# Wide norms at the borders, the norms' weights in front of x's first block, sample softmax one unit later

## The chip, the cores and the metric

The kernel runs on one core of a Trainium2 chip. The metric is the time of one execution on the device in microseconds, as a median of several runs. The profile is of one further execution; its span goes from the first to the last instruction.

Engines are named as in the profile: PE is the matrix engine (PEld its weight loads), DVE the vector engine, ACT the scalar engine, POOL GpSimd, SP the engine that issues most DMAs. An instruction waits in its engine's queue until its operands are ready, and what stands behind it waits too.

## The reference

One inference step of a two-layer encoder with width 1024, for 256 prompt rows and 32 sample rows at once. Each layer has a mixer, a cross-attention into 256 memory tokens and a SwiGLU FFN, each behind an RMSNorm and added to the residual. Cut to what matters here:

```python
def rmsnorm(x, g):
    xf = x.astype(jnp.float32)
    y = xf * lax.rsqrt(jnp.mean(xf * xf, axis=-1, keepdims=True) + RMS_EPS)
    return (y * g.astype(jnp.float32)).astype(x.dtype)

for layer in range(DEPTH):
    ...
    xp = xp + o @ w_out          # o: attention over rmsnorm(xp, g_mix) @ w_in
    xp = xp + memory_attn(rmsnorm(xp, g_xattn[layer]), mk, mv, w_xq[layer], w_xo[layer])
    xp = xp + swiglu(rmsnorm(xp, g_ffn[layer]), w_gate[layer], w_up[layer], w_down[layer])
y_prompt = rmsnorm(xp, g_final)
```

Layer 0's mixer has 8 heads with a relative bias and 8 stick-breaking heads; layer 1's has 16 heads with forget gates. The sample rows attend to caches. All is float32.

## The kernel before

**Layout.** x is held transposed: eight blocks `x[0]` to `x[7]` of 128 features by 288 rows (256 prompt, 32 sample). Every product is made of three fp32r matmuls, because a float32 operand is split into a rounded part and a rest: `hi` and `lo` for weights, `hh` and `hl` for x times the norm's weight (`gain`). ACT makes the rounded part (a CAST, or an ACTIVATE with a scale), DVE the rest. `mm3` issues the three, through `mm` at L68.

**Units.** A unit is one weight tile of 128 x 1024: SP loads it into `st` (4 buffers), ACT casts `hi`, DVE subtracts `lo`, and PE runs 8 x 3 matmuls of 288 columns into one of four accumulators (`acc`, the tile `pj`, `op` or `dn`). Small work (attention, norms, gates) stands between units: generators in `active` are each moved on one step by `tick()` behind a unit, so that a `yield 1` puts what follows it one unit later on PE. Such work uses four other PSUM banks (`att`).

**Norms.** `Norm.add` squares a block on ACT (L251) and adds it up, on POOL but for the last block, which DVE adds (L259). The norm doesn't hold up the projection: PE multiplies the unnormed x, and the result is scaled by `rstd` when it is evacuated. `columns` sums over features with three fp32 matmuls that have the squares as the stationary operand and a column of 1/1024 as the moving one (tile `nrm`), which gives one value per row, rows on partitions; `newton` makes the inverse root of it with 11 DVE instructions of 6 columns (L279 to L284). `rows` spreads it with three fp32 matmuls against `ident` (tile `nr`) over all partitions, and ACT copies it to `rstd` (L331). Evacuations that are asked for earlier wait in `cur.waiting`.

**Borders.** At the border into cross-attention, FFN and layer 1's mixer, `begin` starts two units with the first six blocks of x (18 matmuls each), since the last blocks are still being evacuated. `columns` stands behind the first of the two, and `scale` is a generator that runs `rows` at the first tick.

**Start.** Three weight tiles (`first`, with the blocks in the order of use) and x in four pieces of two blocks (`xh`) are loaded in parts, from SP and ACT's queue; the norms' weights (`gain`, 9 x 8 columns) come in a transfer of their own (L88). PE runs 32 matmuls on an identity (`warm`) meanwhile. `side_by_side` then works on the first three units block by block. Four small constants (`more_constants`) are made on DVE behind the last square.

**Samples and memory.** `attend_sample` makes scores, a softmax (tile `es`), then behind a `yield` transposes it (tile `ts`), and two yields on the result (`os`, `ot`). `Memory.step` makes the memory's keys and values; the values are split into `vh` (ACT) and `vl` (POOL, L371), and the last head's are used in the last attention head of `cross` (tile `xo`).

**End.** The last norm needs no spreading: `columns`, with the squares of the last block summed apart (`hurry`), then transposes `yt`, a scaling by y and the store.

Of the kernel before, what the change touches and what calls it, by code (L numbers as in the profile page):

```python
# [15 lines left out]
P = 128  # L16
# [3 lines left out]
KT = 8  # L20
# [6 lines left out]
def encoder_step(ctx: ExitStack, tc: tile.TileContext, a):  # L27
# [43 lines left out]
    gain = cst.tile([P, 9 * KT], F32, name="gain")  # L71
    xh = [big.tile([P, 2 * NT], F32, tag=f"x{i}", name=f"x{i}") for i in range(4)]
    x = [xh[k // 2][:, (k % 2) * NT:(k % 2) * NT + NT] for k in range(KT)]
# [7 lines left out]
    def x_part(i, eng=DMA):  # L81
        eng.dma_start(xh[i], a["xT"][:, 2 * i * NT:2 * (i + 1) * NT])

    first_part(0, 0, 384)
    x_part(0)
    x_part(1, S)
    x_part(3, S)
    DMA.dma_start(gain, a["gains"])  # L88
    first_part(0, 384, 1024)
    first_part(1, 0, 1024)  # L90
    x_part(2)
    first_part(2, 0, 1024)
# [3 lines left out]
    G.memset(mean1, 1.0 / 1024.0)  # L96
    identb = cst.tile([P, P], BF16, name="identb")
# [3 lines left out]
    line = cst.tile([8, 384], F32, name="line")  # L101
# [38 lines left out]
    def more_constants():  # L140
        V.tensor_scalar(ident, warm[:, 0:P], 1.0 / 32.0, None, op0=ALU.mult)
        by_head = ident.rearrange("p (j i q) -> p j i q", j=2, i=2)
        V.tensor_tensor(fold, by_head[:, :, 0], by_head[:, :, 1], ALU.add)
        V.tensor_tensor(fold4, fold[:, 0, 0:16], fold[:, 1, 0:16], ALU.add)
        V.tensor_copy(ntrir, ntri)
# [95 lines left out]
    class Norm:  # L241
# [7 lines left out]
        def add(self, xb, eng=None):  # L249
# [5 lines left out]
            if self.acc[i] is None:  # L255
                self.acc[i] = q
            else:
                s = tok("ssq")
                eng.tensor_tensor(s[:, :self.n], self.acc[i][:, :self.n], q[:, :self.n], ALU.add)  # L259
                self.acc[i] = s  # L260

        def sum(self, p, part, begin):
            for i, t in enumerate(self.tiles):
                mm(p[:, 2 * i:2 * i + 2], part[:, t:t + 128], mean1, begin and i == 0, False)

        def columns(self, between=None):
            p = att("nrm")
            self.sum(p, self.acc[0], True)
            if between:
                between()  # L270
            if self.acc[1] is not None:
                self.sum(p, self.acc[1], False)
            return self.newton(p)

        def newton(self, p):
            c = len(self.tiles)
            v, y, t = small("ms"), small("y"), small("nt")
            v, y, t = v[:, :2 * c], y[:, :2 * c], t[:, :2 * c]
            V.tensor_scalar(v, p[:, :2 * c], EPS, None, op0=ALU.add)  # L279
            V.tensor_scalar(y.bitcast(I32), v.bitcast(I32), -0.5, 1597463007.0, op0=ALU.mult, op1=ALU.add)  # L280
            for _ in range(3):
                V.tensor_tensor(t, y, y, ALU.mult)
                V.scalar_tensor_tensor(t, t, -0.5, v, op0=ALU.mult, op1=ALU.mult)
                self.last = V.scalar_tensor_tensor(y, t, 1.5, y, op0=ALU.add, op1=ALU.mult)  # L284
            return y

        def rows(self, y):

            p = att("nr")
            for i, t in enumerate(self.tiles):  # L290
                a0 = 256 if i == 2 else t
# [868 lines left out]
```

## Time and profile before

| | us |
|---|---|
| median of 3 runs (957.63 to 958.33) | 957.79 |
| the profiled execution | 958.14 |
| its span | 956.4 |
| PE's idle time in the span (956.4 - 943.6) | 12.8 |
| DVE busy | 587.3 |
| ACT busy | 483.8 |
| POOL busy | 237.2 |

A row of the timeline has the start and the duration of an instruction (or of several that follow each other, xN), its engine, line, operation, output and inputs with their sizes, and in brackets how long the engine was idle before and what ended that. Matmuls overlap, so the cost of one is the distance from one start to the next, not its duration. SPq, POOLq and ACTq are the engines' DMA issues. In the chain of waits a row is start, duration and what held the end up.

### The profile page before, as it was taken

What the parts mean: (1) busy time and instruction counts of PE and PEld (TensorE: products, weight loads), DVE (VectorE), ACT (ScalarE), POOL (GpSimd) and SP (SyncE); (2) the same over time, 40 slices, a digit from 0 to 9 for tenths busy, and PEclk for the clock granted to TensorE, in tenths of its full rate; (3) what the DMA queues carried; (4) which work ended last, traced back from release to release, by engine and by line L of the source; (5) the groups of instructions that cost most, each with busy time, mean ns of one, the idle gap of its engine ahead of it and who ended that gap; (6) DMA issues with size and microseconds to landing.
All of it is one profiled execution on the core that took longest, in us unless ns stands there. A gap on an engine that the chain in (4) does not pass through costs nothing.

```text
span 956.4 us, 19036 instructions
## 1 busy us (share of the span) xinstructions
PE 943.6 (99%) x7476; PEld 915.0 (96%) x7476; DVE 587.3 (61%) x1137; ACT 483.8 (51%) x860; POOL 237.2 (25%) x358
## 2 busy tenths in 40 slices
PE   8999999999999999999999999999999999999997
PEld 8988999999999999999999989999999999999996
DVE  6876556676665555854565666668657655555442
ACT  5666777545554444444455554555445544444431
POOL 4331123400222222410124352432012222222010
PEclk9999999999999999999999999999999999999999
DMA  7665445543444444554466455545425544454431
GB/s 266 208 213 195 155 169 183 183 160 116 142 157 160 171 161 170 176 199 170 160 205 206 168 191 177 184 152 190 139 95 176 168 163 170 162 175 159 174 111 50
DMA packets 49258, 160.97 MB, mean 168 GB/s; under 512 B 7304, under 2 KB 8136, under 8 KB 49168
## 3 DMA queue, kind: packets, MB, share of 16 engines
q1 hardware_dynamic: 44976, 149.12, 45.5%
q0 software_dynamic: 3904, 10.04, 3.0%
q8 instruction: 59, 0.97, 0.4%
q10 hardware_dynamic: 288, 0.59, 0.2%
q14 instruction: 31, 0.25, 0.1%
HBM read 149.58 MB, written 10.15 MB: 167 GB/s over the span
## 4 chain that ended last, share of the span: by engine, by line
PE 84%; issue 11%; DVE 2%; DMA 1%; POOL 1%; ACT 0%; DVEq 0%; SPq 0%; POOLq 0%; ACTq 0%
PE pj L68 49%; PE dn L68 15%; PE op L68 9%; PE mv L68 4%; PE po L68 1%; PE sc L68 1%; PE zb L68 1%; DMA st<-w_ab 1%; DMA gain<-gains 1%; PE nrm L68 0%; PE os L68 0%; POOL ssq L259 0%; PE zs L68 0%; PE nr L68 0%; DVE e L410 0%
## 5 line engine op out<-in xcount | busy, mean ns | idle before, releaser
L156 ACT CAST hi<-st 128x1024 fp32r<-128x1024 f32 x257 | 269.3, 1049 | 312.2 <-issue 140.8
L68 PE MATMUL pj<-hh,hi 128*128 128x288 f32 (+1 forms) x1344 | 400.2, 298 | 1.1 <-ACT hh L299 1.1
L68 PE MATMUL pj<-hl,hi 128*128 128x288 f32 (+1 forms) x1344 | 395.2, 294 | 0.0
L68 PE MATMUL pj<-hh,lo 128*128 128x288 f32 (+1 forms) x1344 | 395.2, 294 | 0.0
L157 DVE TENSOR_TENSOR lo<-st,hi 128x1024 fp32r<-128x1024 f32 x257 | 318.6, 1240 | 94.1 <-PE dn L68 43.0
L68 PEld LDWEIGHTS pj<-hh,hi 128*128 128x128 f32 x1344 | 253.3, 188 | 7.6 <-issue 4.8
L68 PEld LDWEIGHTS pj<-hl,hi 128*128 128x128 f32 x1344 | 253.5, 189 | 0.3 <-DVE hl L302 0.3
L68 PEld LDWEIGHTS pj<-hh,lo 128*128 128x128 f32 x1344 | 253.2, 188 | 0.0
L68 PE MATMUL dn<-fh,hi 128*128 128x288 f32 x400 | 108.8, 295 | 0.0
L68 PE MATMUL dn<-fh,lo 128*128 128x288 f32 x352 | 103.7, 295 | 0.0
L68 PE MATMUL dn<-fl,hi 128*128 128x288 f32 x304 | 89.6, 295 | 0.0
L68 PE MATMUL op<-oh,hi 128*128 128x288 f32 x256 | 76.1, 298 | 0.0
L68 PE MATMUL op<-ol,hi 128*128 128x288 f32 x256 | 75.5, 295 | 0.0
L68 PE MATMUL op<-oh,lo 128*128 128x288 f32 x256 | 75.4, 295 | 0.0
L68 PEld LDWEIGHTS dn<-fh,hi 128*128 128x128 f32 x400 | 72.4, 188 | 0.0
L68 PEld LDWEIGHTS dn<-fh,lo 128*128 128x128 f32 x352 | 66.1, 188 | 0.0
L259 POOL TENSOR_TENSOR ssq<-ssq,sq 128x288 f32<-128x288 f32 (+1 forms) x35 | 34.9, 996 | 120.3 <-ACT sq L251 78.4
L767 POOL TENSOR_TENSOR fl<-us,fh 128x288 fp32r<-128x288 f32 x38 | 33.8, 889 | 120.1 <-ACT fh L766 120.1
L762 DVE TENSOR_TENSOR us<-pj,rstd 128x288 f32<-128x288 f32 x44 | 20.1, 457 | 62.6 <-PE pj L68 62.6
L763 POOL TENSOR_TENSOR gs<-gs,sg 128x288 f32<-128x288 f32 x44 | 39.3, 893 | 72.8 <-ACT sg L761 72.8
L68 PEld LDWEIGHTS dn<-fl,hi 128*128 128x128 f32 x304 | 57.0, 188 | 0.0
L68 PEld LDWEIGHTS op<-oh,hi 128*128 128x128 f32 x256 | 48.0, 188 | 0.7 <-issue 0.4
(268 smaller groups left out, 1255.0 us busy)
## 6 DMA issues: line engine op xcount, KB each, us to landing
st<-w_gate SPq DMA_DIRECT2D x44, 512.0 KB
st<-w_up SPq DMA_DIRECT2D x44, 512.0 KB, 3.2
st<-w_down SPq DMA_DIRECT2D x44, 512.0 KB, 3.2
st<-w_c SPq DMA_DIRECT2D x24, 512.0 KB, 4.0
st<-w_ab SPq DMA_DIRECT2D x21, 512.0 KB, 6.1
st<-w_xk SPq DMA_DIRECT2D x16, 512.0 KB, 4.4
st<-w_xv SPq DMA_DIRECT2D x16, 512.0 KB, 3.8
st<-w_xq SPq DMA_DIRECT2D x16, 512.0 KB, 3.3
```

What stands on the lines that cost most here:

```text
L68: return T.matmul(out, lhsT, rhs, start=start, stop=stop, skip_group_check=True)
L156: a = S.copy(hi, st[:, c0:c1])
L157: b = V.tensor_tensor(lo, st[:, c0:c1], hi.bitcast(F32), ALU.subtract)
L259: eng.tensor_tensor(s[:, :self.n], self.acc[i][:, :self.n], q[:, :self.n], ALU.add)
L762: V.tensor_tensor(us, pu[:, :NT], cur.r, ALU.mult)
L763: G.tensor_tensor(gs, gs, sg, ALU.mult)
L767: G.tensor_tensor(lo, us, hi.bitcast(F32), ALU.subtract)
```

## The change

- **Wide norms at five borders.** `scale` is no generator any more. Within the second unit of `begin`, behind its third block, it calls `wide`: the sum of squares is split into qh (ACT) and ql (DVE), two fp32r matmuls with a 128 x 128 matrix of 1/1024 (`meanr`) sum it over features and leave the mean on all partitions, and `rsqrt` makes `rstd` from it with 8 DVE instructions of 288 columns. The spreading matmuls and ACT's copy are gone there. The evacuations run at once where they are written.
- **The first norm, the memory's and the last** keep `columns`, with the 8 steps of `rsqrt` (two refinements with other constants) in place of 11. EPS is added with the second square, by DVE.
- **Start.** `gain` lies in front of x's first block, in DRAM and in x's first tile; block 0 comes with it in the first transfer on ACT's queue, block 1 on SP. The last third of the weights is loaded in two halves. `ident` is made by ACT, the other constants behind the second projection of the third pair of heads. `line` moves to a work buffer and 32 bytes (`room`) are left free, so that the split weights start at multiples of 256 bytes as before.
- **One more `yield`** between softmax and transposes in `attend_sample`.
- **The last head's `vl`** is made by DVE.

```diff
-    gain = cst.tile([P, 9 * KT], F32, name="gain")
+    xh = [big.tile([P, 2 * NT + (0 if i else 128)], F32, tag=f"x{i}", name=f"x{i}") for i in range(4)]
+    cst.tile([P, 8], F32, name="room")
+    gain = xh[0][:, 0:G0]
...
+    S.dma_start(xh[0][:, 0:G0 + NT], a["xT"][:, 0:G0 + NT])
+    S.dma_start(xh[1], a["xT"][:, G0 + 2 * NT:G0 + 4 * NT])
     first_part(0, 0, 384)
-    x_part(0)
-    x_part(1, S)
-    x_part(3, S)
-    DMA.dma_start(gain, a["gains"])
+    DMA.dma_start(x[1], a["xT"][:, G0 + NT:G0 + 2 * NT])
     first_part(0, 384, 1024)
+    x_part(2)
     first_part(1, 0, 1024)
-    x_part(2)
-    first_part(2, 0, 1024)
+    first_part(2, 0, 512)
+    x_part(3)
+    first_part(2, 512, 1024)
...
                 mm3(p[:, :NT], w, k, cur.h, k, k == 0, False)
+                if out and k == 2:
+                    cur.scale()
             out.append((w, p))
-            if len(out) == 1:
-                cur.y = cur.norm.columns()
...
+            if self.parts == 2:
+
+                V.scalar_tensor_tensor(s[:, :self.n], b, EPS * KT, c, op0=ALU.add, op1=ALU.add)
             else:
...
+        def rsqrt(self, v, y, t, out):
+            V.tensor_scalar(y.bitcast(I32), v.bitcast(I32), -0.5, 1595932665.0, op0=ALU.mult, op1=ALU.add)
+            V.tensor_tensor(t, y, y, ALU.mult)
+            V.scalar_tensor_tensor(t, t, -0.375 * 0.703952253, v, op0=ALU.mult, op1=ALU.mult)
+            V.scalar_tensor_tensor(y, t, 0.375 * 0.703952253 * 2.38924456, y, op0=ALU.add, op1=ALU.mult)
+
+            V.tensor_tensor(t, y, y, ALU.mult)
+            V.scalar_tensor_tensor(t, t, 64.0 / 9.0, v, op0=ALU.mult, op1=ALU.mult)
+            V.scalar_tensor_tensor(t, t, -10.0 / 3.0, t, op0=ALU.add, op1=ALU.mult)
+            self.last = V.scalar_tensor_tensor(out, t, 5.0, y, op0=ALU.add, op1=ALU.mult)
+
+        def wide(self):
+
+            hi, lo = split(self.acc[0], tok("qh", F32R), tok("ql", F32R), V)
+            p = att("nrm")[:, :self.n]
+            mm(p, meanr, hi, True, False)
+            mm(p, meanr, lo, False, True)
+            r = big.tile([P, NT], F32, tag="rstd", bufs=2, name=name("rstd"))
+            self.rsqrt(p, tok("y"), tok("nt"), r)
+            return r
...
         def scale(self):
-
-            if self.gi == 0:
-                yield 1
-            p = self.norm.rows(self.y)
+            self.r, self.waiting = self.norm.wide(), None
...
         softmax(s, [(0, 160)], bias, e)
         yield 1
+        yield 1
         t = att("ts")
...
-                        self.v[t, hd] = split(v[:, 0:NP], tok("vh", F32R)[:, 0:NP], tok("vl", F32R)[:, 0:NP])
+                        self.v[t, hd] = split(v[:, 0:NP], tok("vh", F32R)[:, 0:NP], tok("vl", F32R)[:, 0:NP], V if hd == 3 else G)
...
-            cur.y = cur.norm.columns()
+            start(cur.first_scale())
...
+            if j == 2:
+                more_constants()
...
-    more_constants()
+    S.activation(ident, warm[:, 0:P], AF.Copy, scale=1.0 / 32.0)
...
-        "xT": feats(x), "memT": feats(g["mem_prompt"][0]),
-        "gains": gains.reshape(9, 8, 128).transpose(2, 0, 1).reshape(128, 72),
+        "xT": np.concatenate([gains, feats(x)], axis=1), "memT": feats(g["mem_prompt"][0]),
```

**How the order of work moves.** Three places show it; in the rows, names of tiles carry a number.

PE at the border into layer 0's cross-attention, before: the sums over features (`nrm`) stand ahead of the last matmul of the second unit's first block.

```order
L68 MATMUL pj_2688<-hh_2370,hi_2684 128x288
L68 MATMUL pj_2688<-hl_2371,hi_2684 128x288
L68 MATMUL nrm_2664<-mean_95,ssq_2604 128x2 x3
L68 MATMUL pj_2688<-hh_2370,lo_2685 128x288
L68 MATMUL pj_2688<-hh_2383,hi_2684 128x288
```

The same, 22 matmuls later, where the norm is spread (`nr`):

```order
L68 MATMUL pj_2645<-hl_2599,hi_2641 128x288
L68 MATMUL pj_2645<-hh_2598,lo_2642 128x288
L68 MATMUL nr_2713<-ident,y_2669 128x128 x2
L68 MATMUL nr_2713<-ident,y_2669 128x32
L68 MATMUL pj_2688<-hh_2558,hi_2684 128x288
```

PE there in the change: two wide matmuls on the split sum, behind the third block of the second unit, which is the 27th matmul of the border, and no `nr`.

```order
L68 MATMUL pj_2665<-hl_2394,hi_2661 128x288
L68 MATMUL pj_2665<-hh_2393,lo_2662 128x288
L68 MATMUL nrm_2679<-qh_2675,meanr 128x288
L68 MATMUL nrm_2679<-ql_2676,meanr 128x288
L68 MATMUL pj_2665<-hh_2433,hi_2661 128x288
```

DVE at that border, before, from the last addition of squares to the first evacuation of a query (`xq`), without the six steps between that repeat the three ahead of them:

```order
L302 SCALAR_TENSOR_TENSOR hl_2599<-x_82,gain,hh_2598 128x288
L259 TENSOR_TENSOR ssq_2604<-ssq_2564,sq_2602 128x288
L279 TENSOR_SCALAR ms_2668<-nrm_2664 128x6
L280 TENSOR_SCALAR y_2669<-ms_2668 128x6
L282 TENSOR_TENSOR nt_2670<-y_2669 128x6
L283 SCALAR_TENSOR_TENSOR nt_2670<-nt_2670,ms_2668 128x6
L284 SCALAR_TENSOR_TENSOR y_2669<-nt_2670,y_2669 128x6
...
L157 TENSOR_TENSOR lo_2844<-st_2841,hi_2843 128x1024
L668 SCALAR_TENSOR_TENSOR xq_2719<-pj_2645,rstd_2717 128x288
```

DVE there in the change: `ql`, then eight steps of 288 columns with two weight splits between them.

```order
L270 TENSOR_TENSOR ssq_2599<-ssq_2559,sq_2597 128x288
L389 TENSOR_TENSOR ql_2676<-ssq_2599,qh_2675 128x288
L274 TENSOR_SCALAR y_2683<-nrm_2679 128x288
L275 TENSOR_TENSOR nt_2684<-y_2683 128x288
L276 SCALAR_TENSOR_TENSOR nt_2684<-nt_2684,nrm_2679 128x288
L277 SCALAR_TENSOR_TENSOR y_2683<-nt_2684,y_2683 128x288
L279 TENSOR_TENSOR nt_2684<-y_2683 128x288
L163 TENSOR_TENSOR lo_2833<-st_2830,hi_2832 128x1024
L280 SCALAR_TENSOR_TENSOR nt_2684<-nt_2684,nrm_2679 128x288
L163 TENSOR_TENSOR lo_2890<-st_2887,hi_2889 128x1024
L281 SCALAR_TENSOR_TENSOR nt_2684<-nt_2684 128x288
L282 SCALAR_TENSOR_TENSOR rstd_2682<-nt_2684,y_2683 128x288
```

The norm's steps became wider and fewer, and the splits that stood behind them now stand among them.

ACT at the program's start, before: the first weight piece is cast ahead of the first block of x.

```order
L82 DMA x_80<-xT 128x576
L82 DMA x_82<-xT 128x576
L148 ACT_TABLE_LOAD
L148 ACTIVATE wtab<-mean_95 128x2
L156 CAST hi_177<-first_83 128x384
L299 ACTIVATE hh_183<-x_79,gain 128x288
```

ACT there in the change: the first transfer has 360 columns, the weights of the norms and block 0, and this block comes first.

```order
L88 DMA x_78<-xT 128x360
L89 DMA x_79<-xT 128x576
L154 ACT_TABLE_LOAD
L154 ACTIVATE wtab<-mean_96 128x2
L312 ACTIVATE hh_185<-x_78 128x288
L162 CAST hi_179<-first_83 128x384
```

The cast and the scaling changed places, and block 0 moved from SP's queue to the head of ACT's.

More of the change, by code (lines that the diff above doesn't have):

```diff
@@ L256, in add @@
                 self.acc[i] = q
-            else:
[L258 to L264, printed above, removed]
-        def columns(self, between=None):
[L267 to L273, printed above, removed]
@@ new lines, in wide @@
+        def wide(self):
[6 more added lines that the diff above has]
+            return r
+        def columns(self, between=None):
+            p, tiles = att("nrm"), self.tiles
+            for part in self.acc:
+                if part is not None:
+                    for i, t in enumerate(tiles):
+                        mm(p[:, 2 * i:2 * i + 2], part[:, t:t + 128], mean1, part is self.acc[0] and i == 0, False)
+                if between:
+                    between()
+                between = None
+            y, t = (small(s)[:, :2 * len(tiles)] for s in ("y", "nt"))
+            self.rsqrt(p[:, :2 * len(tiles)], y, t, y)
+            return y
@@ L580, in mem_scales @@
         V.tensor_copy(memcol, y.rearrange("p (t two) -> p t two", two=2)[:, :, 0])
-        S.copy(memrow, memn.rows(y))
+        p = att("nr")
+        for i in range(2):
+            mm(p[:, 128 * i:128 * i + 128], y[:, 2 * i:2 * i + 1].to_broadcast([P, P]), ident, i == 0, True)
+        S.copy(memrow, p[:, :NP])
     class Memory:
@@ L1110, in _pack @@
                       g["g_ffn"][0], g["g_ffn"][1], g["g_final"]])
+    gains = gains.reshape(9, 8, 128).transpose(2, 0, 1).reshape(128, 72)
     w_ab = units(g["w_in_ab"][0])
```

62 lines of the change are left out of this document (27 added, 35 removed).

## The prediction

> **What bounds the kernel now.** I read the page first, then the waits of PE, then the chain and the timeline at the places that the diff touches.
>
> ```profile
> PE 943.6 (99%) x7476; PEld 915.0 (96%) x7476; DVE 587.3 (61%) x1137; ACT 483.8 (51%) x860; POOL 237.2 (25%) x358
> PE 84%; issue 11%; DVE 2%; DMA 1%; POOL 1%; ACT 0%; DVEq 0%; SPq 0%; POOLq 0%; ACTq 0%
> ```
>
> PE is busy 943.6 us of a span of 956.4 us, and it holds 84% of the chain that ended last. So an edit pays in three ways only: it takes instructions from PE's queue, it ends a wait of PE, or it shortens the stretch before PE's first projection or behind its last matmul. The view of PE's waits lists what PE loses between:
>
> ```profile
> PE warm L134 <- POOL identb masks.py:199: 2.6, 1, 2.6
> PE pj L68 <- ACT hh L299: 1.1, 1, 1.1
> PE xo L68 <- POOL vl L371: 1.1, 2, 0.5
> PE ts L463 <- DVE es L410: 0.8, 2, 0.5
> PE sc L68 <- DVE ol L382: 0.3, 1, 0.3
> ...
> 274.99 134.40 PE pj L68 x1014
> ```
>
> After the warm-up loop that is 3.3 us in all. The last row, from the chain of waits, is a stretch with no wait: 1014 matmuls in 134.40 us, so one fp32r matmul of 288 columns costs PE 0.1325 us, and a unit of 24 of them 3.18 us. This row prices what is added to PE.
>
> **The borders.** Five norms (ahead of cross-attention and FFN in both layers, and ahead of layer 1's mixer) become wide. Each loses from PE three fp32 sums and three fp32 spreads (six records each, since the profile counts two for one fp32 matmul) and gains two fp32r matmuls. The chain has three of the five borders; these are the first and the last of them:
>
> ```profile
> 270.71 0.66 PE nrm L68 x6
> 274.40 0.59 PE nr L68 x6
> ...
> 737.28 0.63 PE nrm L68 x6
> 740.97 0.59 PE nr L68 x6
> ```
>
> Removed: 0.66 + 0.59 = 1.25 us and 0.63 + 0.59 = 1.22 us, so about 1.24 us a border. Added: 2 x 0.1325 = 0.265 us. Five borders give 5 x (1.24 - 0.265) = **4.9 us**, if PE doesn't wait for the new operands. Whether it does, I work out at the border ahead of layer 0's FFN:
>
> ```profile
> 267.90 0.30 PE L68 MATMUL pj<-hh,hi 128*128 128x288 f32 x1
> 270.04 0.45 DVE L259 TENSOR_TENSOR ssq<-ssq,sq 128x288 f32<-128x288 f32 x1
> 275.31 0.39 ACT L331 COPY rstd<-nr 128x288 f32<-128x288 f32 x1
> 280.02 0.43 ACT L766 CAST fh<-us 128x288 fp32r<-128x288 f32 x1
> 16.24 1.58 DVE L259 TENSOR_TENSOR ssq<-ssq,sq 128x288 f32<-128x288 f32 x3
> 274.44 1.22 DVE L157 TENSOR_TENSOR lo<-st,hi 128x1024 fp32r<-128x1024 f32 x1 [0.85 <-PE pj L68]
> ```
>
> The last square is added at 270.49. Now its cast to qh follows on ACT (0.43 us, as the cast of fh), directly behind the square in ACT's order, and then ql on DVE (0.45 us, as ssq): ql lies ready near 271.45. On PE the two wide matmuls stand behind 27 matmuls of the border, so they are due at 267.90 + 27 x 0.1325 = 271.48 and 271.61. That is a margin of about 0.15 us; I count no wait, with 0 to 0.3 us a border as bounds.
>
> The other question is rstd, since every evacuation waits for it. Three dependent additions of this shape took 1.58 us on DVE, 0.53 us each. Eight such steps are 4.2 us, and two weight splits of 1.2 us stand between them in DVE's order. From the matmuls' end near 271.9 that gives 271.9 + 4.2 + 2.4 = 278.5, where now it is 275.7: later by 2.8 us. Behind it on DVE wait the evacuations, and for those waits PE's fifth accumulator, of which there are four: due at 267.90 + 0.27 + 4 x 3.18 = 280.9. The slack left is about 2.4 us less one evacuation, so it stays covered. The cross-attention is tighter: PE's first scores come right behind the fourth unit and need two queries evacuated and split (some 2 us on DVE and ACT behind rstd). There I count under 1 us of slack, and keep up to 0.5 us in each layer for the range. The addition of part 2 that goes from POOL to DVE falls some 20 us ahead of the border.
>
> **The start.** These rows carry it:
>
> ```profile
> 0.81 0.90 ACTq L82 DMA_DIRECT2D x<-xT  x2
> 0.82 0.39 SPq L79 DMA_DIRECT2D first<-w_first  x1
> 1.74 0.42 SPq L88 DMA_DIRECT2D gain<-gains  x1
> 2.57 3.60 PE L134 MATMUL warm<-identb 128*128 128x128 bf16 x32 [2.57 <-POOL identb masks.py:199]
> 4.38 0.51 ACT L156 CAST hi<-first 128x384 fp32r<-128x384 f32 x1 [1.14 <-DMA first<-w_first]
> 6.67 0.96 ACT L299 ACTIVATE hh<-x,gain 128x288 fp32r<-128x288 f32 x2 [1.78 <-DMA gain<-gains]
> 7.24 0.95 DVE L302 SCALAR_TENSOR_TENSOR hl<-x,gain,hh 128x288 fp32r<-128x288 f32 x2 [1.76 <-ACT hh L299]
> 7.26 0.61 PE L68 MATMUL pj<-hh,hi 128*128 128x288 f32 x1 [1.10 <-ACT hh L299]
> 10.62 0.45 PE L68 MATMUL pj<-hh,hi 128*128 128x288 f32 x1
> 10.86 0.45 PE L68 MATMUL pj<-hl,hi 128*128 128x288 f32 x1
> 11.32 0.29 PE L68 MATMUL pj<-hh,hi 128*128 128x288 f32 x1
> 11.45 0.29 PE L68 MATMUL pj<-hl,hi 128*128 128x288 f32 x1
> 15.81 0.51 DVE L302 SCALAR_TENSOR_TENSOR hl<-x,gain,hh 128x288 fp32r<-128x288 f32 x1
> 18.88 0.72 PE L68 MATMUL nrm<-mean,ssq 128*128 128x2 f32 x6
> ```
>
> The gains are the third transfer on SP and hold the first hh until 6.67; PE, done with its warm-up at 6.17, waits to 7.26. In the change the gains come with x's first block, 180 KB, first on ACT's queue. The first weight piece, 192 KB and first on SP, was in use at 4.38, so I put the new block there too. Then hh, hi, hl and lo (0.5 us each) are done by about 6.0, and PE runs from its warm-up straight into the projection near 6.2: 1.1 us earlier. If the block landed only when the gains do now, nothing would be won here.
>
> The second effect is speed. PE's spacing is 0.24 us until about 11.2 and 0.13 us from 11.32, 4.0 us behind the unbroken run's start at 7.26. Each of the 14 or so slow matmuls costs 0.11 us more. If the step to the fast spacing needs some 4 us of unbroken work, and PE now works unbroken from 2.57, it comes near 6.6; if it comes at 11.2 whatever PE did, there are even more slow ones, (11.2 - 6.2) / 0.24 = 21 of them. The 72 matmuls, which now end at 18.88, end at 6.2 + 72 x 0.1325 = 15.7 plus 0.11 us for each slow one: near 16.0 in the first case and 18.0 in the second. Gains: 2.9 us and 0.9 us. The feed limits the first case: DVE's last hl ended at 15.81 + 0.51, 9 us behind its first, and with the constants moved out it can hardly end before 14, which with the last nine matmuls allows 15.3; so little room is left. I take **2.4 us**, nearer to the first, since the pause of 1.1 us is what separates the warm-up from the run that became fast.
>
> The Trainium skill's "TensorE: Matmul & The Clock Gate", Part 1, has a rule for this: the array runs at half rate until a free-running window of about 3.4 us was busy. By it the step at 11.2 puts window edges near 7.8 and 4.4, the pause spoiled that window, and without it the fast rate starts near 7.8, with 7 slow matmuls and a gain of 2.4 us; but where the edges lie in another execution is open, so it could also be 1 us more or less. The profile's spacing (0.24 against 0.13 us) agrees with the halving; its clock row doesn't show the slow stretch.
>
> What moves at the start without a price: the four small constants go from DVE's start to the third projection, where DVE is off PE's path, and the identity goes to ACT.
>
> **The waits inside.** The softmax of four samples gets one more unit before its transpose, so es has 3.2 us more: both waits of ts end, **0.8 us**. Their os and ot move back by a unit as well, so each still has a whole unit behind what it needs. What is late next at such a place is the 0.3 us of sc for ol, which stays. For xo the split of the last head's values goes from POOL to DVE:
>
> ```profile
> 242.96 0.56 POOL L231 DMA_DIRECT2D mv<-mv  x1
> 243.54 0.73 POOL L371 TENSOR_TENSOR vl<-mv,vh 128x256 fp32r<-128x256 f32 x1
> 203.37 0.42 DVE L371 TENSOR_TENSOR ql<-xq,qh 128x256 fp32r<-128x256 f32 x1
> ```
>
> On POOL it stands behind the issue of a store (0.56 us) and takes 0.73 us; on DVE the same shape takes 0.42 us with no store ahead. It comes some 0.8 us earlier than now, more than the 0.54 us that PE waited: **1.0 us** in both layers, bounds 0 and 1.1.
>
> **The tail.** The final norm keeps its narrow form, with 8 steps in place of 11:
>
> ```profile
> 947.87 0.17 DVE L279 TENSOR_SCALAR ms<-nrm 128x6 f32<-128x6 f32 x1 [1.31 <-PE nrm L68]
> 949.87 0.17 DVE L284 SCALAR_TENSOR_TENSOR y<-nt,y 128x6 f32<-128x6 f32 x1
> ```
>
> Ten steps of the chain lie between these rows: 0.2 us each. PE has nothing to do here and the outputs wait for y, so three steps fewer are **0.6 us**.
>
> **Sum.** 4.9 + 2.4 + 0.8 + 1.0 + 0.6 = 9.7 us. The profiled execution took 958.14 us (the span and 1.7 us around it), the median is 957.79. 958.14 - 9.7 = 948.4 us; carried to the median, **948.1 us**. The split weights lie at multiples of 256 bytes before and behind, so nothing is counted for their place.
>
> **Rivals.**
> - *The start gives less*: the block with the gains lands late, or the slow spacing lasts to 11.2 anyway. The start term is then 0 to 0.9 us: 949.6 to 950.5 us. For it speaks that no row shows a transfer of this shape. Chance 0.16.
> - *The waits inside come back*: ts, os or xo wait for their buffers or for DVE, whose queue grows. Without the 1.8 us of those two terms it is 949.9 us. Against it: DVE is 61% busy. Chance 0.09.
> - *The border gives nothing*: the change does not free PE, because PE waits for ql as long as the removed matmuls took. That needs ql some 1 us later than worked out, by a weight cast (1.05 us) ahead of qh on ACT or a split ahead of ql on DVE; the order shows neither. 948.1 + 4.9 = 953.0 us. Chance 0.04.
> - *Slower*: the wide chain on DVE holds rstd so long that PE runs out of accumulators. It decides at five borders beyond the 2.4 us of slack; to eat 9.7 us each border must lose 1.9 us, so rstd must come 4.3 us later than I have it, or a wide step take 1.07 us in place of 0.53. At 1.2 us a step, 8 x 0.67 = 5.4 us later, PE would lose 3.0 us at each: 948.1 + 15 = 963.1 us. Against it stand the rows of 0.45 and 0.53 us. Chance 0.04.
>
> **How the numbers follow.** The forecast has 0.67, with 946.0 to 949.6 as its own range (the start up to 2.9 and a little more, waits of 0.3 us at each border the other way). 0.2% of this kernel is 1.9 us, about what a measurement can tell from no change. Faster by more: the forecast and the first two rivals, and most of the third, 0.93; within: 0.03; slower: 0.04. To hold 8 in 10, the range goes over the first two rivals: 945.8 to 951.5 us.
>
> **What would show it.** Each step has its row in the profile after: no nr group at the five borders and two wide nrm matmuls 0.13 us apart, with no row "PE nrm <- DVE ql" among PE's waits; no row "PE pj <- ACT hh", and the 72 first matmuls ending near 16.5; no rows of ts and xo among the waits; eight steps of 0.2 us ahead of the last scaling. PE's waits on "DVE rstd" or on evacuations within 15 us of a border would make the forecast wrong, and so would a new wait of PE for weights (DVE lo) in the first 30 us, where the projection now asks for them earlier.

## The result and the profile after

| | before | after |
|---|---|---|
| median of 4 runs, us | 958.06 (957.63 to 958.68) | 950.56 (950.46 to 950.66) |
| profiled execution, us | 958.14 | 950.66 |
| its span, us | 956.4 | 949.0 |

The ratio of the times is 0.9921, with a 95% interval of 0.9906 to 0.9937: 7.5 us faster. The forecast was 948.1, which is 9.7 us faster: the sum was 2.2 us too large. (In run 9 below, one of the four executions had only 0.75 of the clock from start to end; it is left out, and since it is the profiled one, that run shows no rows.)

First the page of the kernel after, the busy times and the shares of the chain that ended last:

```profile
PE 938.2 (99%) x7426; PEld 908.6 (96%) x7426; DVE 598.7 (63%) x1129; ACT 483.8 (51%) x861; POOL 224.4 (24%) x347
PE 96%; DMA 1%; DVE 1%; ACT 1%; issue 0%; DVEq 0%; SPq 0%; ACTq 0%
```

PE is busy 938.2 us where it was 943.6, so 5.4 of the 7.5 us by which the span is shorter are work that PE no longer does, or does faster. Idle stayed 10.8 of the 12.8 us. The view of PE's waits says where (what waited, for whom, us in total, times, longest):

```profile
PE warm L140 <- POOL identb masks.py:199: 2.6, 1, 2.6
PE gc L68 <- DVE lf L953: 1.3, 1, 1.3
PE zb L68 <- ACT vn L409: 0.3, 1, 0.3
PE sc L68 <- ACT vn L409: 0.2, 1, 0.2
PE pj L68 <- DVE lo L163: 0.2, 1, 0.2
```

All four rows of before behind the warm-up are gone (hh 1.1, vl 1.1, es 0.8, ol 0.3: 3.3 us); for the first three that was forecast, while ol was forecast to stay. But four new ones of 2.0 us stand there, one of them large: the gate of layer 1's mixer waits for lf. The view does not show everything, so I measured the same stretches of PE's timeline in both kernels, from row to row, and set the forecast beside them:

| stretch on PE | before, us | after, us | gain | forecast |
|---|---|---|---|---|
| start of the span to the end of the first 72 matmuls | 18.88 | 16.35 | 2.53 | 2.4 |
| from there to the border into cross-attention (layer 0's mixer) | 171.79 | 172.27 | -0.48 | 0.4 |
| border to the first scores xs | 14.15 | 12.94 | 1.21 | 0.98 |
| xs to the projection behind the first samples' scores | 6.16 | 7.00 | -0.84 | 0 |
| on to the transpose xsp (holds the wait for vl) | 35.87 | 35.06 | 0.81 | 0.5 |
| on to layer 1's mixer (holds FFN's border) | 232.40 | 231.00 | 1.40 | 0.98 |
| border and gate of layer 1's mixer, to the first vt | 35.92 | 36.14 | -0.22 | 0.98 |
| the rest of the mixer | 141.91 | 142.18 | -0.27 | 0.4 |
| layer 1: border to xs | 14.19 | 12.98 | 1.21 | 0.98 |
| xs to the projection behind the samples' scores | 6.16 | 6.98 | -0.82 | 0 |
| on to xsp | 35.94 | 35.10 | 0.84 | 0.5 |
| on to the last norm (holds FFN's border) | 232.13 | 230.72 | 1.41 | 0.98 |
| last norm to the end | 10.93 | 10.23 | 0.70 | 0.6 |
| sum | 956.43 | 948.95 | 7.48 | 9.7 |

So borders and vl brought more than forecast; 3.7 us were lost at three kinds of places: the gate (1.28), the samples' scores (1.66) and the mixers (0.75). Here are the rows of each.

**The start** in the kernel after:

```profile
4.66 0.54 ACT L312 ACTIVATE hh<-x 128x288 fp32r<-128x288 f32 x1 [1.42 <-DMA x<-xT]
5.92 0.59 PE L68 MATMUL pj<-hh,hi 128*128 128x288 f32 x1
16.35 0.79 PE L68 MATMUL nrm<-mean,ssq 128*128 128x2 f32 x6
```

The first block is scaled 2.0 us earlier than before (6.67), and PE goes from its warm-up into the projection at 5.92, where it waited until 7.26.

**A border** (FFN, layer 0), PE's timeline before (start, duration, instruction):

```profile
270.55 0.82 PE L68 MATMUL nrm<-mean,ssq 128*128 128x2 f32 x6
271.24 0.38 PE L68 MATMUL pj<-hh,lo 128*128 128x288 f32 x1
271.45 0.30 PE L68 MATMUL pj<-hh,hi 128*128 128x288 f32 x1
271.59 0.29 PE L68 MATMUL pj<-hl,hi 128*128 128x288 f32 x1
```

and after, with the rows of DVE that hang on it:

```profile
267.74 0.46 DVE L389 TENSOR_TENSOR ql<-ssq,qh 128x288 fp32r<-128x288 f32 x1 [0.50 <-ACT qh L388]
268.23 0.29 PE L68 MATMUL nrm<-qh,meanr 128*128 128x288 f32 x1
268.36 0.29 PE L68 MATMUL nrm<-ql,meanr 128*128 128x288 f32 x1
268.49 0.29 PE L68 MATMUL pj<-hh,hi 128*128 128x288 f32 x1
274.16 0.46 DVE L282 SCALAR_TENSOR_TENSOR rstd<-nt,y 128x288 f32<-128x288 f32 x1
274.65 0.46 DVE L780 TENSOR_TENSOR gs<-pj,rstd 128x288 f32<-128x288 f32 x1
```

The two wide matmuls take 0.26 us of PE. ql ends at 268.20, 0.03 us ahead of the first: no wait, but hardly a margin (the forecast worked with 0.15). Of before, look at the distances of the starts: nrm takes 271.24 - 270.55 = 0.69 us, and the fp32r matmul behind it 0.21 us to the next start, where the others take 0.13. The same 0.08 us stands behind nr. This is what the forecast left out: an fp32 group also slows the matmul behind it.

**The samples' scores** in layer 0's cross-attention, before and then after:

```profile
209.41 0.65 PE L684 MATMUL xt<-ident,xe 128*128 128x128 f32 x4
209.98 1.06 PE L68 MATMUL xss<-ca,xq 128*32 128x256 f32 x8
210.98 0.40 PE L68 MATMUL pj<-hh,hi 128*128 128x288 f32 x1
```

```profile
206.01 0.30 PE L68 MATMUL pj<-hh,lo 128*128 128x288 f32 x1
206.31 0.30 PE L705 MATMUL xt<-ident,xe 128*128 128x128 f32 x1
206.54 0.62 PE L68 MATMUL xss<-ca,xq 128*32 128x256 f32 x2
207.09 0.55 PE L705 MATMUL xt<-ident,xe 128*128 128x128 f32 x3
207.57 1.06 PE L68 MATMUL xss<-ca,xq 128*32 128x256 f32 x6
208.56 0.40 PE L68 MATMUL pj<-hh,hi 128*128 128x288 f32 x1
```

The same instructions stand in another order: one score matmul (two records) has come between the first and the other three transposes. The stretch takes 2.25 us in place of 1.57, and ahead of it lies a gap of 0.17 us that no wait row shows. No term of the sum had this place. The rows also say where most of the 0.68 us goes: the six records that are left take as long as the eight did (208.56 - 207.57 = 0.99 us, and 210.98 - 209.98 = 1.00), so the one that stands alone costs its whole 0.55 us. Record by record, the eight of before start as four pairs, 0.01 us apart within a pair and 0.2 us from pair to pair; after, only two such pairs are left, and four records start alone.

**The gate**, PE's rows in layer 1's mixer, before and after:

```profile
489.66 0.71 PE L68 MATMUL gt<-fold,gz 128*128 128x16 f32 x6
500.86 0.82 PE L68 MATMUL gc<-tri,lf 128*16 128x256 f32 x4
```

```profile
485.97 0.68 PE L68 MATMUL gt<-fold,gz 128*128 128x16 f32 x6
493.94 0.82 PE L68 MATMUL gc<-tri,lf 128*16 128x256 f32 x4 [1.28 <-DVE lf L953]
```

Between the two stands a chain of small operations on DVE and ACT, up to lf at 493.89. Before, 11.2 us of matmuls covered it; now there are 8.0 us, 1.28 of them waiting. `scale` was a generator, and the gate began when its first step had run; now `cur.then` runs at once and the gate begins one step earlier, so that one of the four steps up to gc is the short rest of a unit begun ahead (6 matmuls) and not a whole one.

### The profile page after: what moved, and what is told of

Same layout as the page of the kernel before. It is cut to its first block, busy times and chain, and to the rows that moved or that the text cites. A ratio compares the mean times of both kernels' runs of the same rounds, so it can differ in the third digit from the quotient of the medians.

```text
span 949.0 us, 18931 instructions
## 1 busy us (share of the span) xinstructions
PE 938.2 (99%) x7426; PEld 908.6 (96%) x7426; DVE 598.7 (63%) x1129; ACT 483.8 (51%) x861; POOL 224.4 (24%) x347
## 4 chain that ended last, share of the span: by engine, by line
PE 96%; DMA 1%; DVE 1%; ACT 1%; issue 0%; DVEq 0%; SPq 0%; ACTq 0%
PE pj L68 55%; PE dn L68 15%; PE op L68 11%; PE mv L68 5%; PE po L68 1%; PE xs L68 1%; PE xo L68 1%; PE sc L68 1%; PE zb L68 1%; PE xss L68 1%; DMA st<-w_ab 1%; DMA first<-w_first 1%; PE xt L705 0%; PE os L68 0%; PE zs L68 0%; PE nrm L68 0%
```

## The experiments

Each edit is to the kernel after unless it says otherwise. Each run was timed beside the kernel before on its own chip (958.3 to 958.4 there).

**1. The gate's sum one step later.**

```diff
-        for _ in range(4):
+        for _ in range(5):
             yield 1
         c = att("gc")
```

> The changed kernel with one step more between the gate's projection and its cumulative sum in layer 1's mixer. My theory: the wide norm lets the gate start one step earlier, its chain of small operations has one unit of matmuls less to lie beside, and PE waits 1.28 us for lf (row PE gc <- DVE lf). With one step more the row is gone and the time is 949.3 us (950.56 - 1.28). Rival: the gate is late because rstd is late on DVE, and what stands behind it only moves; then PE waits for the biases or the scores behind the gate instead, and the time stays at 950.5 us.

Measured: 950.81 us (949.44 to 951.56), ratio 0.9918 (0.9904 to 0.9932). The row for lf is gone, gc stands 9.1 us behind gt, and the stretch from gt to the first vt is 1.35 us shorter than in the kernel after. The place says what the theory said, and so does the fastest execution (949.3 was expected); the median doesn't. In the profiled execution, 951.56 us, the loss lies elsewhere, near 75 us, where layer 0's mixer is 2.3 us longer than in the kernel after:

```profile
75.05 1.04 ACT L162 CAST hi<-st 128x1024 fp32r<-128x1024 f32 x1 [2.76 <-DMA st<-w_xk]
76.52 0.25 ACT L409 COPY vn<-vt 32x128 f32<-32x128 f32 x1
76.83 0.92 PE L68 MATMUL zb<-q,kv 64*128 64x256 f32 x4 [1.17 <-ACT vn L409]
```

On ACT a weight cast waits 2.76 us for its weights to land; vn stands behind it; PE waits 1.17 us for vn. In the kernel after the same cast begins at 74.23 and PE waits 0.3 us. How late this cast begins differs from profile to profile, and 2 us behind the wait, from 78.94 to 82.35, the matmuls also run at the slow spacing (0.21 us). Before, PE waited 0.47 us for es near this place.

**2. The samples' scores ahead of the transposes.**

```diff
             if hd % 2 == 1:
-                active.append(sample(hd // 2))
+                active.insert(0 if hd == 1 else len(active), sample(hd // 2))
```

> The changed kernel with the samples' score matmuls (xss) of the first pair ahead of the first head's four transposes (xt) in both cross-attentions, so that no xss matmul stands between two xt. My theory: what the change lost there (PE took 2.25 us from the first xt to the next projection, where it took 1.57 us before, and waited 0.17 us ahead of it) comes from the mixed order, and PE no longer waits for xe: 0.85 us in each layer, so 948.9 us (950.56 - 1.7). Rival: the loss is a wait for xe alone, which the profile doesn't list; the four xt then wait behind the xss no longer either, and the stretch is 1.6 us as well, so this run alone doesn't tell these two apart (the next one does). Third: the pieces cost the same in any order, and the time stays at 950.5 us.

Measured: 949.97 us (949.10 to 951.05), ratio 0.9911 (0.9898 to 0.9925): two executions near the 948.9 that was expected, two well above. From xs to the next projection PE takes 6.08 and 6.09 us in the two layers, where the kernel after has 7.00 and 6.98: 1.8 us in all, in a profiled span of 947.5.

**3. The order of before at this place**, with the next projection held behind it too (`turned[0]` is the last of the four xt).

```diff
-                    mm(s[32 * i:32 * i + 32, 0:256], qs[4 * g + 2 * i + f][:, 256:288], ck[i][:, 256 * f:256 * f + 256], f == 0, f == 1)
+                    not_before(mm(s[32 * i:32 * i + 32, 0:256], qs[4 * g + 2 * i + f][:, 256:288], ck[i][:, 256 * f:256 * f + 256], f == 0, f == 1), turned[0])
...
+                if turned[0]:
+                    not_before(i, turned[0])
```

> The changed kernel with the order of before at the same place: four xt, four xss, then the next projection. If the mixed order cost the time, the stretch from the first xt on is 1.6 us as before, and PE waits at most 0.3 us for the second half of xe: 0.4 to 0.7 us less in each layer, 949.2 to 949.8 us. If the wait for xe cost it, the stretch stays near 2.3 us and the time near 950.5 us.

Measured: 951.35 us (949.97 to 951.81), ratio 0.9927 (0.9913 to 0.9940). xs to the projection takes 6.39 and 6.37 us: from xt on it is 1.64 us, where the kernel after has 2.25, and the gap of 0.17 us ahead of xt stays. So of the 0.84 us a layer, some 0.6 are the mixed order and 0.2 the gap. The gap is a wait for xe by the rows of the kernel after: the first half of xe ends on DVE at 206.16, and xt follows at 206.31; with xss ahead (run 2) it isn't lost. The median doesn't show 1.2 us, with executions 1.8 us apart; the profiled one, at 949.97, does show about half of it.

**4. The extra unit taken out again.**

```diff
         softmax(s, [(0, 160)], bias, e)
         yield 1
-        yield 1
         t = att("ts")
```

> The changed kernel without the one unit more ahead of the sample softmax's transposes. By the prediction's term PE waits again for es, twice, 0.8 us in all: 951.4 us. By the places read from the trace since then (the first two samples' stretch gained nothing: where ts and os moved, PE now waits 0.25 us twice for ACT vn, and each small group that stands by itself costs a little), the part is worth about nothing: 950.3 to 950.8 us, with ts <- es back among the waits and the rows of vn gone.

Measured: 951.67 us (950.40 to 952.55), ratio 0.9928 (0.9916 to 0.9941). The rows of vn go and PE waits for es (1.4 us, once) and for ol (0.5 us). Against the kernel after, layer 0's mixer is 0.45 us longer and layer 1's 0.44 us shorter, so by these two profiles the extra unit is worth nothing; the fastest executions agree (950.40 and 950.46), and the medians lie 1.1 us apart, with executions 2.2 us apart. The 0.8 us of the forecast are not to be seen: near 75 us PE waits for another tile in place of es, and why layer 1's mixer lost is not shown. Another 1.5 us of this profile are found behind the gate's wait:

```profile
494.68 0.82 PE L68 MATMUL gc<-tri,lf 128*16 128x256 f32 x4 [1.28 <-DVE lf L952]
...
496.86 0.42 PE L68 MATMUL pj<-hl,hi 128*128 128x256 f32 x1
497.08 0.42 PE L68 MATMUL pj<-hh,lo 128*128 128x256 f32 x1
...
499.85 0.37 PE L68 MATMUL pj<-hh,hi 128*128 128x256 f32 x1
500.06 0.28 PE L68 MATMUL pj<-hl,hi 128*128 128x256 f32 x1
500.18 0.28 PE L68 MATMUL pj<-hh,lo 128*128 128x256 f32 x1
```

From 496.56 to 500.06 the matmuls stand 0.21 us apart, then 0.12. The view by windows has the clock for it; first this run, then the kernel after, which had the same wait of 1.28 us without the slow stretch, then the slow stretch of this run alone (window, length and PE busy, granted clock, DMA's share, GB/s):

```profile
495.00:500.00 5.00, 5.00 (x30) 0.66 0.46 142
```

```profile
495.00:500.00 5.00, 5.00 (x44) 1.00 0.43 143
```

```profile
496.62:500.04 3.42, 3.42 (x17) 0.50 0.63 204
```

**5. The kernel after once more**, on the chip of runs 6 to 8, as their measure.

> The changed kernel once more, on the chip of the other runs of this call, as their measure. 950.5 us in the executions in which no stretch of matmuls runs at the slow spacing; 1.5 to 1.9 us more in those in which one does, as the run with one unit less had behind PE's wait for lf (16 matmuls 0.21 us apart instead of 0.12).

Measured: 951.16 us (950.49 to 952.15), ratio 0.9926 (0.9914 to 0.9938). Its fastest execution is that of the first measurement; the others are up to 1.7 us slower.

**6. Narrow norms at the borders, the rest as changed.** The code of before for `columns` in `begin` and `scale` as a generator, with the new eight steps.

```diff
+            if len(out) == 1:
+                cur.y = cur.norm.columns()
-                if out and k == 2:
-                    cur.scale()
...
+        active.append(cur.scale())
```

> The changed kernel with the narrow norms of before at the five borders (with the new eight steps); start, softmax and vl as changed. The scheduler's order at the first scores of cross-attention is then that of before, and the gate starts one step later again. By what I read from the two traces the five borders gain 1.1 to 1.5 us each, 6.2 us, and the wide norm gives back 1.3 us at the gate and 1.7 us at the samples' scores: 3.2 us net, so 953.7 us, without the row PE gc <- DVE lf and with xt four in a row. By the prediction's term (4.9 us and nothing back): 955.4 us. Rival: the order and the gate's wait come from another part, and stay: 956.7 us.

Measured: 955.08 us (954.06 to 956.50), ratio 0.9965 (0.9953 to 0.9977): 3.9 us slower than run 5 by the medians, 3.6 by the fastest executions. xs to the projection takes 6.16 us in both layers, with the four xt in a row; gc stands 11.2 us behind gt with no row for lf; borders into cross-attention take 14.16 and 14.22 us, as before. So the mixed order and the gate's wait come from the wide norm, and the rival that has them elsewhere (956.7) is out. The net price lies nearer to 3.2 us than to the forecast's 4.9.

**7. The kernel before with 42 warm-up matmuls** in place of 32.

```diff
-    for i in range(32):
-        warmed = T.matmul(warm[:, 0:P], identb, identb, start=i == 0, stop=i == 31)
+    for i in range(42):
+        warmed = T.matmul(warm[:, 0:P], identb, identb, start=i <= 10, stop=i < 10 or i == 41)
```

> The kernel before, with 42 warm-up matmuls instead of 32, so that PE works unbroken until its first projection at 7.26 us; nothing else is moved. If the pause of 1.1 us is what brought the slow spacing (0.24 us until 11.2), the projection starts at the fast one: 14 matmuls by 0.11 us, 1.4 us faster than before (956.6 where before has 958.1). If the fast spacing comes at 11.2 whatever PE did, or some time behind the first projection, nothing changes.

Measured: 957.77 us (957.06 to 958.56) beside 958.29, ratio 0.9992 (0.9984 to 1.0001): 0.5 us where 1.4 was expected, and hardly clear of no change. PE still paused 0.38 us, and the fast spacing is there two matmuls behind the pause, at 8.38. But the 72 matmuls end at 18.24, only 0.64 us earlier: PE now waits for hl, whose feed ends no sooner. So with a shorter pause the fast spacing came earlier, in this one profile, and still that is worth only 0.64 of the 2.53 us; the rest, it follows, comes from the earlier feed.

**8. The kernel after with 16 warm-up matmuls**, and the identity that is made from them scaled by 1/16.

```diff
-    for i in range(32):
+    for i in range(16):
```

> The changed kernel with 16 warm-up matmuls instead of 32: PE pauses from about 4.4 us to 5.9. If the fast spacing needs unbroken work, it comes 3.4 to 4.0 us behind the first projection, near 9.6, instead of at 6.54: 13 to 15 more slow matmuls by 0.11 us, 1.4 to 1.6 us slower than the changed kernel. If the step is at a fixed time, nothing changes.

Measured: 953.62 us (951.08 to 955.70), ratio 0.9952 (0.9938 to 0.9966); 2.5 us slower than run 5 by the medians, 0.6 by the fastest executions, of which the profiled one is one. There the fast spacing comes at 9.41 and the 72 matmuls end at 16.98, 0.63 us later than in the kernel after. Twelve slow matmuls more are 1.3 us, of which half is hidden: PE began 0.38 us earlier, and it had been ahead of its feed. The other executions, up to 955.70 us, lose more than the start can give; where isn't shown.

**9. Both repairs**, the edits of 1 and 2.

> The changed kernel with both repairs: the gate's sum one step later, and the samples' scores ahead of the transposes in both cross-attentions. If the two losses are apart from each other, 1.28 + 1.7 = 3.0 us faster than the changed kernel: 947.5 us. The rows PE gc <- DVE lf and the mixed xt and xss are gone; a wait for ACT vn near 75 us, which differs from run to run (0.3 to 1.2 us), stays. If one hides the other, 948.5 to 949.

Measured: 947.78, 949.49 and 950.84 us; ratio 0.9907 (0.9892 to 0.9922). Only the lowest is near the 947.5 that was expected; the middle one lies 2.0 us above it, where the expectation had 948.5 to 949 for losses that hide each other. So this run doesn't show that the two repairs add up; the next one does, by its stretches.

**10. Both repairs, and the memory's blocks read one unit earlier.**

```diff
-            if self.l == 0:
-                yield 1
             for c in range(2):
```

> The kernel of the run ahead, with the memory's blocks read one unit earlier (they hold two of the four buffers that the weights land in; near 70 us the weights of the memory's keys are issued late for it, and the cast that waits for them on ACT stands ahead of vn, for which PE waits). If that is the cause of PE's wait for vn near 75 us, the row PE zb <- ACT vn is gone and the time is 0.3 to 1 us under the run ahead. If the wait is ACT's own work, it stays.

Measured: **946.39 us** (946.27 to 946.42), ratio 0.9876 (0.9861 to 0.9891): the fastest of all, 4.2 us below the kernel after, in four executions within 0.15 us. PE's waits are these two:

```profile
PE warm L140 <- POOL identb masks.py:199: 2.6, 1, 2.6
PE pj L68 <- DVE lo L163: 0.2, 1, 0.2
```

The late cast of weights is done ahead of time, ACT is free when vt is there, and PE no longer waits for vn:

```profile
73.31 1.05 ACT L162 CAST hi<-st 128x1024 fp32r<-128x1024 f32 x1 [1.71 <-issue]
74.89 0.37 ACT L408 COPY vn<-vt 128x256 f32<-128x256 f32 x1 [0.26 <-PE vt L406]
```

Its stretches against the kernel after: 0.9 us at the samples' scores of each layer, 1.4 at the gate, about 0.6 up to 77 us.

**11. The wide chain doubled**: eight steps more on DVE at each of the five borders. They only write values that the last step writes over.

```diff
+            for _ in range(8 if out.shape[-1] == NT else 0):
+                V.tensor_tensor(out, t, y, ALU.mult)
             self.last = V.scalar_tensor_tensor(out, t, 5.0, y, op0=ALU.add, op1=ALU.mult)
```

> The changed kernel with eight more wide steps on DVE ahead of the last step of each of the five wide norms (their values are written over), so rstd comes 8 x 0.49 = 3.9 us later: the rival that ends slower, at a measured size. Slack read from the trace: 0.6 us at the first scores of cross-attention, about 2.7 us at FFN's fifth accumulator, none at the gate. PE should wait 3.3 us twice, 1.2 us twice and 3.9 us more at the gate: 13 us, 963.5 us; 1.5 us more for each stretch of slow matmuls that such a wait brings. If the slack were what the prediction had for FFN at all five places (2.4 us), 5 x 1.5: 958 us.

Measured: 975.34 us (974.55 to 977.22), ratio 1.0181 (1.0167 to 1.0195). Slower than any theory had it; the three largest rows of PE's waits:

```profile
PE pj L68 <- DVE xq L691: 6.7, 2, 3.4
PE pj L68 <- DVE gs L782: 6.7, 2, 3.4
PE pj L68 <- DVE q L817: 2.7, 1, 2.7
```

and what stands at FFN's border of layer 0:

```profile
287.17 0.46 DVE L284 SCALAR_TENSOR_TENSOR rstd<-nt,y 128x288 f32<-128x288 f32 x1
287.67 0.46 DVE L782 TENSOR_TENSOR gs<-pj,rstd 128x288 f32<-128x288 f32 x1
288.18 0.61 PE L68 MATMUL pj<-hh,hi 128*128 128x288 f32 x1 [3.35 <-DVE gs L782]
288.58 0.44 PE L68 MATMUL pj<-hl,hi 128*128 128x288 f32 x1
...
293.62 0.43 PE L68 MATMUL pj<-hl,hi 128*128 128x288 f32 x1
293.86 0.33 PE L68 MATMUL pj<-hh,lo 128*128 128x288 f32 x1
```

The border begins at 271.70, and rstd ends 15.93 us later; in the kernel after it is 274.62 - 264.65 = 9.97 us. So it is 5.96 us later: 3.9 for the steps, and the rest for two more weight splits that DVE's order puts in between. The fifth accumulator is due 13.0 us behind the border's beginning, and its evacuation is done 0.5 us behind rstd: a slack of 13.0 - 9.97 - 0.5 = 2.5 us in the kernel after, and 5.96 - 2.5 = 3.5 us of waiting here. So the slack at FFN is about as the prediction had it, and the expectation of 1.2 us of waiting failed because it moved rstd by the steps alone. At cross-attention PE waits 3.4 us, near the 3.3 expected, and at the mixer 2.7 us for q and not 3.9 at the gate; both times it is the next projection that waits for an evacuation. Then come the stretches behind the waits: here 22 starts 0.24 us apart, 2.4 us more, with a granted clock of 0.50 from 287.09 to 293.91. The span is 26.5 us longer than that of the kernel after; the five waits are 16.2 us of it, and such stretches, which the expectation left out of its 13 us, are the largest part of the rest: one behind each of the five waits, and a sixth behind a wait of 1.0 us for vn.

**12. vl on POOL again.**

```diff
-tok("vl", F32R)[:, 0:NP], V if hd == 3 else G)
+tok("vl", F32R)[:, 0:NP])
```

> The changed kernel with the split of the last head's values on POOL again. PE then waits 0.5 us for vl in each layer as before, and the one projection matmul between the first and second half of xo is no longer needed: 0.8 us in each layer by the places read from the two traces, 952.1 us; by the prediction's term 951.5 us. Rival: the store's issue on POOL sets the time and stands ahead in either case, so nothing changes: 950.5 us.

Measured: 954.35 us (952.27 to 955.59), ratio 0.9954 (0.9942 to 0.9967). PE waits 1.1 us for vl in two places. In layer 0 the twelve xo take 2.24 us; without the waits, and without the one matmul of the output projection that stands between them, they take 1.45: 0.79 us. Layer 1 reads 0.8 us. The fastest execution is 1.8 us above that of the kernel after; the profiled one also has a slow stretch behind the gate's wait (1.5 us).

## Why the prediction was right, and where it was wrong

- **What bounds the kernel** held: PE's queue and PE's waits. Each gain and each loss above is on PE.
- **"Five borders give 4.9 us"**: right in mechanism at the border itself, and too small in the term "Removed: 1.24 us a border". By the rows, 0.69 + 0.58 us for the two groups and 0.08 us for the slowed matmul behind each, less 0.26: 1.17 us, so 5.9 us for five. Four borders read 1.2 to 1.4 us in the table. No wait for ql came, by 0.03 us.
- **"The slack left is about 2.4 us less one evacuation"** at FFN, so 1.9: 2.5 by rows. The end of rstd lies 9.97 us behind the border's beginning, where the prediction's rows of before have 275.70 - 267.90 = 7.80; it moved by 2.2 us and not by 2.8. Run 11 bears the slack out. It also shows that the rival that ends slower was a real one: it decides at about 2.5 us, and its price is higher than worked out, because PE's slow stretch comes on top of each wait.
- **What failed is that the border was priced as if only its own instructions moved.** I worked out by how much rstd moves and asked who waits for it, but not what the generator's end does to the gate. That a step of the scheme went away made the gate begin one step earlier, and PE wait 1.28 us for lf (runs 1 and 10 take it away, run 6 too). The wide norm also changed the order in which xt and xss are issued: 0.84 and 0.82 us (runs 2, 3, 6). Together they are 2.9 us that no term had. That the order changed by the later rstd is argued, not shown: run 11, with rstd another 6 us later, has the same mixed order. The order of the instructions, known ahead of the run, shows the mixed xt and xss; the prediction used it for the norm's rows only.
- **The start, 2.4 us**: measured 2.53. PE began at 5.92, near the 6.2 of the forecast. But one of the two reasons was wrong: I tied the gain to the point at which the fast spacing comes (near 6.6 or 11.2). In the profiled executions of kernels with the new start and the full warm-up it came anywhere from the first matmuls to 8.47, and the 72 matmuls ended between 16.30 and 16.68 all the same: the feed sets the end, as the text feared for the first case. Shortening the pause alone brings 0.64 us (run 7). One of the signs of being wrong that I had named did show, a new wait for weights in the first 30 us: the row for lo, at 10.18. It is 0.2 us and changes nothing.
- **ts, 0.8 us**: both rows went, and the stretches lost 0.75 us together. The wait near 75 us went from es to vn. Behind vn stands a cast whose weights came late (run 1), and with the memory's blocks read earlier it is gone (run 10). For es no row shows late weights: before, its exponential ends on ACT at 71.48 and its reciprocal begins on DVE at 72.34, behind a weight split of 1.21 us that starts at 71.20. The rival "the waits inside come back" had this in part.
- **xo, 1.0 us**: measured 0.81 and 0.84, 1.65 us, and 0.79 by run 12. The row of 0.54 us is less than what the wait costs PE: five xo take 0.59 us by themselves, and the sixth came 1.30 us behind the first, so 0.71 us, and the rest is the slow start behind it.
- **The tail, 0.6 us**: measured 0.70.

By the table, the forecast was 2.3 us too small at the borders (1.4, with what else lies in FFN's stretches), xo (0.65), the start (0.13) and the tail (0.1), and 4.5 us too large at the gate (1.28), the order (1.66) and the mixers (0.75 lost where 0.8 was to be won). The difference is the 2.2 us between 9.7 and 7.5. That the sum came as near as this is in part luck, since errors of 4.5 and 2.3 us went against each other. The measured 950.56 lies outside the forecast's own range of 946.0 to 949.6; the stated range holds it only because it was stretched over two rivals, and neither is what happened: the start gave all that was forecast, and PE's waits for es and vl went.

## What to carry to other kernels

When an edit takes a step out of a scheme of steps, list all that counts in those steps and ask how many matmuls still lie beside each chain: what was hidden by four whole units may be hidden by three and a quarter. Read the new order along the whole stretch in which the moved result is used, not only where it is made. And find the root of a wait before paying for it: here a unit more ended the wait for es, and PE waited for vn instead, behind a cast whose weights came late.

## What the runs showed of the hardware

- **A wait of PE can cost more than its length.** Behind waits of 1.02 to 1.28 us PE sometimes ran at half speed for 3.4 us: from 78.94 to 82.35 in run 1, from 496.62 to 500.04 in run 4, from 496.92 to 500.33 in run 12 and from 78.88 to 82.28 in run 11 (the wait of 1.02), each with a granted clock of 0.50 and matmuls 0.21 us apart in place of 0.12. It costs about 1.5 us. The kernel after and runs 2, 3, 5 and 8 had the same wait of 1.28 us without it, and what decides is not shown: in the 3.4 us that hold the wait, PE is busy 2.13 us in run 4 and 2.14 us in the kernel after. Behind the waits of 2.7 to 3.4 us in run 11 the clock was 0.50 each time, four times for 3.4 us and once for 6.8.
- **That such stretches spread the executions of one kernel is argued.** The mean clock of each execution speaks for it in part: in run 8 it falls from 0.999 at 951.08 us to 0.996 at 955.70, in run 9 from 0.998 at 947.78 to 0.996 at 950.84. Against it, all five executions of run 5 have 0.998 and lie 1.7 us apart, and the kernel after had 0.20 us between its four executions in the first measurement, hardly more than the 0.15 of run 10, which has no such wait.
- The Trainium skill's "TensorE: Matmul & The Clock Gate", Part 1, states a free-running window of 3.4 us after which the rate is set anew. The length of the stretches agrees, and so does the step at the start, which came at different times with the same program. Its section "Why this matters for your kernels" counts gaps above about 3 us as harmful; here gaps of 1.02 to 1.28 us were enough in some executions, and the measurement decides.
- **An fp32 group slows the fp32r matmul behind it**: 0.21 us to the next start in place of 0.13, behind nrm and behind nr.
- **Matmuls of few columns can lose their partners.** The score matmuls (128x32 stationary) start in pairs 0.01 us apart when the eight records stand together; with one matmul moved between the transposes, six records took the time of eight, and the place cost some 0.6 us (run 3 against the kernel after).
